# A two-layer encoder trunk on one core: the values' product ahead of the stick-breaking q and k, transposes issued in three steps, the last sparse heads two steps later

## The chip, the core and the metric

The kernel runs on one core of a Trainium2 chip. Its engines work side by side, each through its own queue of instructions in order: TensorE (PE in the profile, with its weight loads as PEld), VectorE (DVE), ScalarE (ACT), GpSimd (POOL) and SyncE (SP, which here issues DMA transfers). The metric is the device time of one execution in microseconds (us).

## What is computed

Two layers. In each, one input projection feeds three mixers over the 256 tokens: forgetting attention (fox, 6 heads), stick-breaking attention (sb, 5 heads) and sparse attention (dsa, 5 heads, whose keys an indexer with 8 heads selects). Sigmoid gates merge them, a projection and a feed-forward part follow. Cut to what matters here:

```python
h = x @ w_in[i]
(fq, fk, fv, ff_logit, sq, sk, sv, dq, dk, dv, iq, ik, iw, g) = split_cols(h)
o_fox = fox_attention(fq, fk, fv, log_f)
o_sb = stick_breaking_attention(sq, sk, sv)
dq, dk, iq, ik = (rope(a, pos) for a in (dq, dk, iq, ik))
o_dsa = dsa_attention(dq, dk, dv, iq, ik, iw)
gates = jax.nn.sigmoid(g.reshape(b, s, N_BRANCH, D_MODEL))
merged = (gates[:, :, 0] * (o_fox @ w_up_fox[i])
          + gates[:, :, 1] * (o_sb @ w_up_sb[i])
          + gates[:, :, 2] * (o_dsa @ w_up_dsa[i]))
x = layer_norm(DEEPNORM_ALPHA * x + merged @ w_out[i], ln1_g[i], ln1_b[i])
ffn = jnp.square(jax.nn.relu(x @ w_ff_in[i])) @ w_ff_out[i]
ple = jax.nn.sigmoid(x @ w_ple_gate[i]) * (p[i] @ w_ple[i])
x = layer_norm(DEEPNORM_ALPHA * x + ffn + ple, ln2_g[i], ln2_b[i])
```

## The kernel before

**Numbers in two halves.** Every operand of a product is written as a high and a low half (`split`): ScalarE rounds to the high half (L181), VectorE subtracts to get the low half (L182), or both scale on the way. A product is then three matmuls (`mm3`, L197 and the like): high by high, high by low, low by high. Weights come in units: a DMA brings a unit to a raw buffer `wr` (3 of them), the two engines split it to `wh` and `wl` (5 of each).

**Accumulators.** PSUM has eight banks: four under the name `ps`, for scores, transposes and values, and four under the name `pg`, for the products of the input projection and the up projection. `xstat` keeps the tokens still and takes two `pg` banks, one per half of the tokens (tile 0, tile 1); `wstat` keeps the weights still and takes a bank for every two blocks of 128 columns: three for `fox` (6 heads) and three for `sb` (its q and k, L407 to L410). Each name gives its banks out in a ring, so that a new accumulator waits until the bank's last content was read. When a product ends, its `done` function evacuates the banks: `c4_done` (dsa), `c3_done` (sv), `sb_done`. The first two call `do_rope`, which multiplies on VectorE into two temporary buffers, of which there are two in all (`t15`; L369, L371, L373), adds on GpSimd (L376), and splits the values after that.

**The order of the work.** `PRODUCTS` lists the products; `JOBS` lists the mixers' generators, each with the number of rounds until the next may start. In a round, every job in flight (up to FLIGHT = 6) is advanced by one step, that is, to its next `yield`; then jobs whose products are done are started, and then the products run on by about PACE = 550 columns. So a `yield` within a job puts a piece of a product between its parts. A scheduler places the instructions of each engine on from this order.

**The jobs the change touches.** `idx_T` (L485 to L497) transposes the indexer's keys and its two blocks of queries and splits them. `dsa_T` (L560 to L575) does so for the keys of the sparse heads, for four query heads in one bank, and for the fifth query head. `dsa1` and `dsa3` are `softmax_heads` for two sparse heads each: scores (L204), softmax, transposes of the weights (L217), splits, and `values` (L197 into `ps`), whose output is split into `oT` (L592, L593).

**The end of the mixers.** When all jobs are through, `zero` (L885) is computed from the last softmax tile. It is the bias of the sigmoids of the twelve gate tiles (L888), so that ScalarE loads the sigmoid's table only there. `gated` (L762) multiplies accumulators of the up projection (`up`, L758 to L831; its units `kbs` of two blocks kb) by the gates and thereby frees their `pg` banks. Then the output projection (L251) follows.

Of the kernel before, what the change touches and what calls it, by code (L numbers as in the profile page):

```python
# [27 lines left out]
BIG = 1e30  # L28
TAKEN = -3e38

PRODUCTS = ['fv', 'fox', 'iq1', 'iq2', 'dsa', 'sb', 'sv', 'g1', 'g2', 'g3', 'g4', 'g5']
JOBS = [('decay', 4), ('fox0', 2), ('fox2', 2), ('fox4', 1), ('idxT', 1), ('idx0', 3), ('idx1', 0), ('dsaT', 2), ('sb0', 2), ('sb2', 2), ('dsa0', 0), ('sb4', 2), ('dsa1', 0), ('dsa3', 4)]
PACE = 550
FLIGHT = 6
WR = 3
# [16 lines left out]
def hybrid_trunk(ctx, tc, x, p, w_in, b_forget, w_up_fox, w_up_sb, w_up_dsa, w_out,  # L52
# [10 lines left out]
    def nm(s):  # L63
        uid[0] += 1
        return f"{s}_{uid[0]}"

    def ps():
        return psp.tile([P, 512], F32, tag="ps", name=nm("ps"), bufs=4)
# [109 lines left out]
    def split(src, hi, lo, scale=None):  # L178

        if scale is None:  # L180
            a = nc.scalar.copy(hi, src)  # L181
            b = nc.vector.tensor_sub(lo, src, hi.bitcast(F32))  # L182
            if pinned[0]:
                pinned[0] -= 1
                tc.keep_in_program_order(a)
                tc.keep_in_program_order(b)
        else:
            nc.scalar.activation(hi, src, AF.Copy if isinstance(scale, float) else AF.Identity,
                                 scale=scale)
            nc.vector.scalar_tensor_tensor(lo, src, scale, hi.bitcast(F32),  # L190
                                           op0=ALU.mult, op1=ALU.subtract)
# [166 lines left out]
    for l in range(L):  # L358
# [126 lines left out]
        def idx_T():  # L485
            q = ps()
            for t in range(2):
                nc.tensor.transpose(q[:, t * P:(t + 1) * P], rnk[t][:, 0:128], ident)
            split(q[:, 0:256], *ikT)
            for g in range(2):  # L490
                q = ps()
                for b in range(2):
                    for t in range(2):
                        nc.tensor.transpose(q[:, b * T + t * P:b * T + (t + 1) * P],
                                            rnq[t][:, (2 * g + b) * P:(2 * g + b + 1) * P], ident)
                split(q, *iqT[g])
            yield  # L497
# [62 lines left out]
        def dsa_T():  # L560
            q = ps()
            for t in range(2):
                nc.tensor.transpose(q[:, t * P:(t + 1) * P], rnk[t][:, 128:256], ident)
            split(q[:, 0:256], *dkT)
            q = ps()
            for b in range(2):
                for t in range(2):
                    nc.tensor.transpose(q[:, b * T + t * P:b * T + (t + 1) * P],
                                        rnd[t][:, b * P:(b + 1) * P], ident)
            split(q, *dqT, scale=-SCALE)  # L570
            q = ps()
            for t in range(2):
                nc.tensor.transpose(q[:, t * P:(t + 1) * P], rnd[t][:, 256:384], ident)
            split(q[:, 0:256], *dq4, scale=-SCALE)
            yield  # L575
# [264 lines left out]
        for c in range(1, 6):  # L840
            products[f"g{c}"] = (KB, 512, lambda c=c: gate(c))

        jobs = {"decay": (("fv",), lambda: decay()), "idxT": (("iq1", "iq2"), idx_T),
                "idx0": (("iq1", "iq2"), lambda: idx_scores(0)),
                "idx1": (("iq1", "iq2"), lambda: idx_scores(1)),
                "dsaT": (("dsa", "sv"), dsa_T)}
        for h in (0, 2, 4):
            jobs[f"fox{h}"] = (("fox", "fv"), lambda h=h: fox_heads(h))
# [7 lines left out]
        def gemm():  # L856
            for name in PRODUCTS:
                _, n, f = products[name]
                for _ in f():
                    yield n  # L860
                emitted.add(name)

        units, todo, more = gemm(), list(JOBS), True
        while more or todo or flight:
# [181 lines left out]
```

## Time and profile before

| what | us |
|---|---|
| three runs, lowest, median, highest | 884.89, 891.12, 891.59 |
| profiled execution, its own time | 887.57 |
| its span in the trace | 885.9 |
| TensorE busy | 859.0 (97% of the span) |
| VectorE busy | 643.3 (73%) |
| ScalarE busy | 475.7 (54%) |
| GpSimd busy | 72.0 (8%) |
| mean granted clock of TensorE | 0.993 of full speed |

The span is the time from the first to the last instruction of the profiled execution; 1.7 us lie around it. Busy shares are means over the whole span. The granted clock is 1.00 at 2.4 GHz and 0.50 at 1.2 GHz. TensorE's busy time counts a matmul from its start to its modelled end, so that neighbours overlap.

### The profile page before, as it was taken

The numbers are of one execution on the slowest core, as the hardware profiler recorded it, in microseconds if no ns is written. First come the engines' busy times: TensorE is split into PE (matmuls) and PEld (weight loads), VectorE is DVE, ScalarE is ACT, GpSimd is POOL, SyncE is SP. The second block draws the span as 40 slices with busy tenths as digits, with TensorE's granted clock in tenths as the row PEclk, the third lists the DMA queues.
The fourth block names the chain that finished last, engine by engine and source line by source line (L and its number), as shares of the span: only waits on it lengthen the run. The fifth ranks groups of instructions, "written<-read, shape, count | busy, mean of one in ns | idle before, by whom it ended". The sixth has DMA issues, their size and how long they took to land. (4 is left out here: it accounts for less than half of the span.)

```text
span 885.9 us, 12952 instructions
## 1 busy us (share of the span) xinstructions
PE 859.0 (97%) x4678; PEld 733.3 (83%) x4678; DVE 643.3 (73%) x1133; ACT 475.7 (54%) x749; POOL 72.0 (8%) x138
## 2 busy tenths in 40 slices
PE   7998999999999999999999989999999999999996
PEld 5998978788788888888879988887887888888885
DVE  5588897779867666666776799967798686666665
ACT  4555657676445444444455556676844554444440
POOL 2012011100011000000000122001001010000100
PEclk9999999999999999999999999999999999999998
DMA  7654566543556666666546547554355666566751
GB/s 232 196 149 124 160 183 187 157 154 117 177 186 208 215 190 190 190 214 213 156 119 201 145 128 198 160 173 149 106 192 188 179 205 210 191 189 188 230 179 48
DMA packets 79696, 154.46 MB, mean 174 GB/s; under 512 B 10096, under 2 KB 25456, under 8 KB 79632
## 3 DMA queue, kind: packets, MB, share of 16 engines
q1 hardware_dynamic: 77952, 149.04, 55.0%
q0 software_dynamic: 1680, 4.60, 1.9%
q8 instruction: 37, 0.61, 0.3%
q14 instruction: 27, 0.22, 0.1%
HBM read 152.30 MB, written 1.05 MB: 173 GB/s over the span
## 5 line engine op out<-in xcount | busy, mean ns | idle before, releaser
L182 DVE TENSOR_TENSOR wl<-wr,wh 128x1024 fp32r<-128x1024 f32 (+5 forms) x303 | 344.2, 1142 | 185.8 <-ACT wh L181 183.1
L181 ACT CAST wh<-wr 128x1024 fp32r<-128x1024 f32 (+5 forms) x303 | 296.2, 983 | 298.3 <-PE pg L197 83.3
L197 PE MATMUL pg<-wh,t16k 128*128 128x512 f32 (+4 forms) x768 | 224.6, 367 | 0.1
L945 PE MATMUL ps<-t16k,wh 128*128 128x512 f32 x512 | 181.4, 398 | 0.0
L197 PE MATMUL pg<-wh,t2k 128*128 128x512 f32 x544 | 172.8, 394 | 1.7 <-ACT wh L181 1.4
L197 PEld LDWEIGHTS pg<-wh,t16k 128*128 128x128 f32 x768 | 140.6, 189 | 20.0 <-DVE t2k L190 0.7
L947 PE MATMUL ps<-t16k,wl 128*128 128x256 f32 x512 | 143.7, 281 | 0.0
L197 PE MATMUL pg<-wl,t16k 128*128 128x512 f32 (+4 forms) x384 | 139.5, 363 | 0.0
L197 PEld LDWEIGHTS pg<-wh,t2k 128*128 128x128 f32 x544 | 102.9, 189 | 24.2 <-ACT wh L181 1.8
L945 PEld LDWEIGHTS ps<-t16k,wh 128*128 128x128 f32 x512 | 96.2, 188 | 23.8
L197 PE MATMUL pg<-wl,t2k 128*128 128x512 f32 x272 | 106.7, 392 | 0.0
L947 PEld LDWEIGHTS ps<-t16k,wl 128*128 128x128 f32 x512 | 96.7, 189 | 0.6
L197 PEld LDWEIGHTS pg<-wl,t16k 128*128 128x128 f32 x384 | 72.7, 189 | 8.1
L197 PEld LDWEIGHTS pg<-wl,t2k 128*128 128x128 f32 x272 | 51.5, 189 | 10.9 <-DVE wl L182 0.5
L407 PE MATMUL pg<-t16k,wh 128*128 128x256 f32 x176 | 51.3, 291 | 3.7 <-DVE t16k L182 3.7
L409 PE MATMUL pg<-t16k,wh 128*128 128x256 f32 x176 | 50.5, 287 | 0.0
L410 PE MATMUL pg<-t16k,wl 128*128 128x256 f32 x176 | 50.4, 286 | 0.0
L251 PE MATMUL pg<-wh,t16k 128*128 128x512 f32 x96 | 37.6, 398 | 1.3 <-ACT t16k L181 1.2
L251 PE MATMUL pg<-wl,t16k 128*128 128x512 f32 x96 | 37.9, 399 | 0.8 <-DVE wl L182 0.6
L407 PEld LDWEIGHTS pg<-t16k,wh 128*128 128x128 f32 x176 | 34.3, 195 | 4.3 <-issue 4.1
L197 PE MATMUL pg<-wh,t1k 128*128 128x512 f32 x112 | 37.2, 396 | 0.0
L410 PEld LDWEIGHTS pg<-t16k,wl 128*128 128x128 f32 x176 | 34.5, 196 | 0.0
(180 smaller groups left out, 969.5 us busy)
## 6 DMA issues: line engine op xcount, KB each, us to landing
wr<-in_w_ff_in_dram SPq DMA_DIRECT2D x64, 512.0 KB, 4.4
wr<-in_w_ff_out_dram SPq DMA_DIRECT2D x64, 512.0 KB, 4.2
wr<-in_w_in_dram SPq DMA_DIRECT2D x48, 512.0 KB, 4.0
wr<-in_w_in_dram SPq DMA_DIRECT2D x32, 384.0 KB, 3.4
wr<-in_w_out_dram SPq DMA_DIRECT2D x16, 512.0 KB, 4.1
wr<-in_w_ple_gate_dram SPq DMA_DIRECT2D x16, 512.0 KB, 4.5
wr<-in_w_in_dram SPq DMA_DIRECT2D x16, 256.0 KB, 3.4
wr<-in_w_in_dram SPq DMA_DIRECT2D x8, 390.0 KB, 3.7
```

The source lines that it names most:

```text
L181: a = nc.scalar.copy(hi, src)
L182: b = nc.vector.tensor_sub(lo, src, hi.bitcast(F32))
L197: nc.tensor.matmul(o, l, r, start=start and i == 0, stop=stop and i == 2, skip_group_check=skip)
L251: nc.tensor.matmul(o[t][:, :n], tok(aT, u * nk + kk, t)[0], wt[i][:, kk, :], start=u + kk + i == 0, stop=False)
L407: nc.tensor.matmul(oi, hi, rh, start=kb == 0 and i % 2 == 0, stop=False, skip_group_check=True)
L409: nc.tensor.matmul(oi, hi, rl, start=False, stop=False, skip_group_check=True)
L410: nc.tensor.matmul(oi, lo, rh, start=False, stop=kb == KB - 1, skip_group_check=True)
L945: nc.tensor.matmul(pz[i], hi, x1_both[:, kb, :], start=kb == 0, stop=False, skip_group_check=True)
L947: nc.tensor.matmul(pz[i][:, 0:T], lo, x1T[0][:, kb, :], start=False, stop=kb == KB - 1, skip_group_check=True)
```

## The change

`PRODUCTS` puts `sv` (the stick-breaking values, with the first query head of the sparse mixer behind them) ahead of `sb` (the stick-breaking q and k). `idx_T` and `dsa_T` get two more `yield`s each, so that each of their three transposed banks is a step of its own. In `JOBS` two rounds instead of one lie between `idxT` and `idx0`, and two instead of none between `dsa1` and `dsa3`. Nothing else changes; lines after the new ones move by one to three (L494 is L495 after, L573 is L576, L593 is L596, L762 is L765, L779 is L782, L888 is L891).

```diff
--- before.py
+++ after.py
@@ -28,8 +28,8 @@
 BIG = 1e30
 TAKEN = -3e38
 
-PRODUCTS = ['fv', 'fox', 'iq1', 'iq2', 'dsa', 'sb', 'sv', 'g1', 'g2', 'g3', 'g4', 'g5']
-JOBS = [('decay', 4), ('fox0', 2), ('fox2', 2), ('fox4', 1), ('idxT', 1), ('idx0', 3), ('idx1', 0), ('dsaT', 2), ('sb0', 2), ('sb2', 2), ('dsa0', 0), ('sb4', 2), ('dsa1', 0), ('dsa3', 4)]
+PRODUCTS = ['fv', 'fox', 'iq1', 'iq2', 'dsa', 'sv', 'sb', 'g1', 'g2', 'g3', 'g4', 'g5']
+JOBS = [('decay', 4), ('fox0', 2), ('fox2', 2), ('fox4', 1), ('idxT', 2), ('idx0', 3), ('idx1', 0), ('dsaT', 2), ('sb0', 2), ('sb2', 2), ('dsa0', 0), ('sb4', 2), ('dsa1', 2), ('dsa3', 4)]
 PACE = 550
 FLIGHT = 6
 WR = 3
@@ -488,6 +488,7 @@
                 nc.tensor.transpose(q[:, t * P:(t + 1) * P], rnk[t][:, 0:128], ident)
             split(q[:, 0:256], *ikT)
             for g in range(2):
+                yield
                 q = ps()
                 for b in range(2):
                     for t in range(2):
@@ -562,12 +563,14 @@
             for t in range(2):
                 nc.tensor.transpose(q[:, t * P:(t + 1) * P], rnk[t][:, 128:256], ident)
             split(q[:, 0:256], *dkT)
+            yield
             q = ps()
             for b in range(2):
                 for t in range(2):
                     nc.tensor.transpose(q[:, b * T + t * P:b * T + (t + 1) * P],
                                         rnd[t][:, b * P:(b + 1) * P], ident)
             split(q, *dqT, scale=-SCALE)
+            yield
             q = ps()
             for t in range(2):
                 nc.tensor.transpose(q[:, t * P:(t + 1) * P], rnd[t][:, 256:384], ident)
```

**First place: sb's third accumulator in layer 0.** On TensorE before; `pg_1087`, `pg_1088` and `pg_1089` are the three banks of sb, `ps_1138` is the second block of the indexer's queries.

```order
L494 MATMUL ps_1138<-ident,t2k_302 128x128
L494 MATMUL ps_1138<-ident,t2k_303 128x128
L494 MATMUL ps_1138<-ident,t2k_302 128x128
L407 MATMUL pg_1089<-t16k_195,wh_1093 128x256
L409 MATMUL pg_1089<-t16k_195,wh_1093 128x256
L410 MATMUL pg_1089<-t16k_195,wl_1094 128x256
L494 MATMUL ps_1138<-ident,t2k_303 128x128
L407 MATMUL pg_1087<-t16k_195,wh_1148 128x256
```

On TensorE in the changed kernel; sb's banks are `pg_1226` to `pg_1228`, `ps_1257` is the indexer's second block of queries, and L204 are the first scores of the indexer.

```order
L217 MATMUL ps_1251<-ident,t3k_1008 128x128 x3
L495 MATMUL ps_1257<-ident,t2k_302 128x128
L495 MATMUL ps_1257<-ident,t2k_303 128x128
L495 MATMUL ps_1257<-ident,t2k_302 128x128
L495 MATMUL ps_1257<-ident,t2k_303 128x128
L407 MATMUL pg_1228<-t16k_195,wh_1232 128x256
L409 MATMUL pg_1228<-t16k_195,wh_1232 128x256
L410 MATMUL pg_1228<-t16k_195,wl_1233 128x256
L204 MATMUL ps_1265<-t1k_308,t2k_310 128x128
L204 MATMUL ps_1266<-t1k_308,t2k_310 128x128
```

Before, the last accumulator of sb is opened among the transposes of the second query block; after, behind all of them, and the indexer's scores stand right behind the unit's last matmuls.

On VectorE before, at the evacuation that this accumulator waits for; `pg_919` is the bank of tile 0 of the dsa product:

```order
L625 TENSOR_SCALAR t3k_1008<-t3k_1008,small_1118 128x128
L625 TENSOR_SCALAR t3k_1008<-t3k_1008,small_1118 128x256
L369 TENSOR_TENSOR t_212_1059<-pg_919,rope 128x64
L371 TENSOR_TENSOR t_213_1060<-pg_919,rope 128x32
L373 TENSOR_TENSOR t_213_1060<-pg_919,rope 128x32
L182 TENSOR_TENSOR wl_1261<-wr_1257,wh_1260 128x640
L182 TENSOR_TENSOR t16k_210<-pg_919,t16k_210 128x64
```

On VectorE in the changed kernel; `pg_1087` and `pg_1088` are the two banks of the sv product there:

```order
L369 TENSOR_TENSOR t_240_1206<-pg_1087,rope 128x64
L371 TENSOR_TENSOR t_241_1207<-pg_1087,rope 128x32
L373 TENSOR_TENSOR t_241_1207<-pg_1087,rope 128x32
L369 TENSOR_TENSOR t_242_1216<-pg_1088,rope 128x64
L371 TENSOR_TENSOR t_243_1217<-pg_1088,rope 128x32
L373 TENSOR_TENSOR t_243_1217<-pg_1088,rope 128x32
L182 TENSOR_TENSOR wl_1384<-wr_1380,wh_1383 128x640
L182 TENSOR_TENSOR t16k_210<-pg_1087,t16k_210 128x320
L182 TENSOR_TENSOR t16k_210<-pg_1088,t16k_210 128x320
L182 TENSOR_TENSOR t3k_1174<-ps_1251,t3k_1173 128x384
L182 TENSOR_TENSOR t2k_313<-ps_1257,t2k_312 128x512
```

Before, tile 0's value split (`t16k_210`) is the last of this row. After, the ropes of both tiles come first, then the low half of a weight unit, then both value splits, then the split of a softmax tile, and last that of the indexer's second query block.

**Second place: the end of the mixers in layer 0.** On ScalarE before; `wh_...` are the high halves of weight units, `t3k_...` those of softmax tiles, and `small_2337` is `zero`.

```order
L181 CAST wh_2423<-wr_2419 128x1024
L181 CAST t3k_2245<-ps_2282 128x384
L181 CAST t3k_2253<-ps_2288 128x384
L181 CAST wh_2442<-wr_2439 128x1024
L888 ACT_TABLE_LOAD
L888 ACTIVATE t2k_259<-t2k_259,small_2337 128x512
L181 CAST t1k_334<-ps_2315 64x256
```

On ScalarE in the changed kernel:

```order
L181 CAST t1k_334<-ps_2280 64x256
L181 CAST wh_2442<-wr_2439 128x1024
L181 CAST t3k_2291<-ps_2320 128x384
L181 CAST wh_2477<-wr_2474 128x1024
L891 ACT_TABLE_LOAD
L891 ACTIVATE t2k_259<-t2k_259,small_2337 128x512
L181 CAST t1k_336<-ps_2326 64x256
```

Before, one weight unit (`wh_2442`) is rounded between the last softmax tile and the table load; after, one stands ahead of the last softmax tile and another (`wh_2477`) behind it. That one takes the buffer of `wh_2357`.

On TensorE before, the matmuls of the up projection there; `pg_2307` and `pg_2308` are its second pair of accumulators, `pg_2383` and `pg_2384` its third, which kb = 6 opens:

```order
L197 MATMUL ps_2326<-t3k_2253,t16k_210 128x2x128
L197 MATMUL pg_2307<-wh_2357,t1k_330 128x512
L197 MATMUL pg_2307<-wl_2358,t1k_330 128x512
L197 MATMUL pg_2307<-wh_2357,t1k_331 128x512
L197 MATMUL pg_2308<-wh_2357,t1k_330 128x512
L197 MATMUL pg_2308<-wl_2358,t1k_330 128x512
L197 MATMUL pg_2308<-wh_2357,t1k_331 128x512
L779 MATMUL pg_2307<-wh_2357,t1k_332 128x512
L780 MATMUL pg_2307<-wl_2358,t1k_332 128x512
L779 MATMUL pg_2308<-wh_2357,t1k_332 128x512
L780 MATMUL pg_2308<-wl_2358,t1k_332 128x512
L779 MATMUL pg_2383<-wh_2379,t1k_333 128x512
```

On TensorE in the changed kernel, `pg_2312` and `pg_2313` are the second pair, `pg_2383` is again the first of the third:

```order
L197 MATMUL ps_2326<-t3k_2291,t16k_210 128x512
L782 MATMUL pg_2312<-wh_2357,t1k_332 128x512
L783 MATMUL pg_2312<-wl_2358,t1k_332 128x512
L782 MATMUL pg_2313<-wh_2357,t1k_332 128x512
L783 MATMUL pg_2313<-wl_2358,t1k_332 128x512
L197 MATMUL ps_2326<-t3k_2292,t16k_210 128x512
L197 MATMUL ps_2326<-t3k_2291,t16k_210 128x512
L197 MATMUL ps_2326<-t3k_2291,t16k_210 128x2x128
L197 MATMUL ps_2326<-t3k_2292,t16k_210 128x2x128
L197 MATMUL ps_2326<-t3k_2291,t16k_210 128x2x128
L782 MATMUL pg_2383<-wh_2379,t1k_333 128x512
```

Before, all values of the last heads (`ps_2326`) stand ahead of the last matmuls of the second pair; after, most of them stand between those and the third pair, and `wh_2357` is read last at the fourth row of this piece.

## Rows read from the trace of the kernel before

**Rows 1.** Windows, both mixer stretches: busy us (instructions) per engine, clock, DMA share, GB/s.

```profile
55.00:252.00 197.00, 190.96 (x1091) 162.17 (x1090) 163.23 (x360) 118.49 (x211) 23.52 (x41) 0.99 0.54 160
489.00:690.00 201.00, 195.67 (x1119) 166.58 (x1118) 165.57 (x364) 122.24 (x217) 23.63 (x41) 0.99 0.53 158
```

**Rows 2.** Waits of TensorE: line, releaser, us in total, times, longest us.

```profile
PE pg L407 <- DVE t16k L182: 3.7, 2, 1.9
PE ps L204 <- DVE t1k L593: 3.1, 2, 1.5
PE ps L573 <- DVE t1k L182: 2.0, 2, 1.2
...
PE pg L251 <- DVE wl L182: 0.6, 2, 0.4
```

**Rows 3.** Timeline, sb's third accumulator, layer 0: start, us, [idle before <-releaser].

```profile
81.25 0.28 PE L410 MATMUL pg<-t16k,wl 128*128 128x256 f32 x1
81.37 0.49 PE L217 MATMUL ps<-ident,t3k 128*128 128x128 f32 x3
...
81.92 0.93 PE L494 MATMUL ps<-ident,t2k 128*128 128x128 f32 x7
84.67 0.36 PE L407 MATMUL pg<-t16k,wh 128*128 128x256 f32 x1 [1.83 <-DVE t16k L182]
```

**Rows 4.** Windows around three clock levels, columns as in rows 1.

```profile
85.67:89.08 3.41, 3.41 (x18) 3.41 (x17) 2.61 (x8) 1.95 (x5) 1.70 (x5) 0.50 0.31 89
521.00:524.50 3.50, 3.50 (x32) 3.50 (x31) 3.04 (x11) 2.61 (x5) 1.88 (x6) 1.00 0.39 98
611.32:614.73 3.41, 3.41 (x9) 2.67 (x8) 3.34 (x20) 2.68 (x12) 0.00 (x0) 0.50 0.71 219
```

**Rows 5.** Timeline at the last sparse scores of layer 0.

```profile
174.87 0.77 DVE L593 TENSOR_TENSOR t1k<-ps,t1k 64x256 fp32r<-64x256 f32 x2
...
175.35 0.32 PE L204 MATMUL ps<-t1k,t2k 64*128 64x128 f32 x1 [1.54 <-DVE t1k L593]
```

**Rows 6.** Timeline at the end of layer 0's mixers.

```profile
192.53 0.39 PE L197 MATMUL pg<-wh,t1k 128*128 128x512 f32 x1
...
192.76 2.25 PE L197 MATMUL ps<-t3k,t16k 128*128 128x512 f32 x12
...
193.00 1.05 ACT L181 CAST wh<-wr 128x1024 fp32r<-128x1024 f32 x1 [1.60 <-issue]
194.07 1.28 ACT L888 ACT_TABLE_LOAD   x1
...
195.37 0.72 ACT L888 ACTIVATE t2k<-t2k,small 128x512 f32<-128x512 f32 x1
...
196.12 0.69 DVE L762 TENSOR_TENSOR t2k<-pg,t2k 128x512 f32<-128x512 f32 x1 [0.81 <-ACT t2k L888]
...
197.35 0.39 PE L780 MATMUL pg<-wl,t1k 128*128 128x512 f32 x1
...
197.79 0.50 PE L779 MATMUL pg<-wh,t1k 128*128 128x512 f32 x1
```

**Rows 7.** Timeline at the end of the sv product, layer 0.

```profile
111.73 0.51 PE L197 MATMUL pg<-wh,t16k 128*128 128x384 f32 x2
...
112.08 0.33 PE L197 MATMUL pg<-wl,t16k 128*128 128x384 f32 x1
...
113.17 0.21 DVE L369 TENSOR_TENSOR t<-pg,rope 128x64 f32<-128x64 f32 x1
...
113.67 1.22 POOL L376 TENSOR_TENSOR t2k<-t,t 128x64 f32<-128x64 f32 x1 [5.75 <-DVE t L373]
...
114.63 0.48 DVE L182 TENSOR_TENSOR t16k<-pg,t16k 128x320 fp32r<-128x320 f32 x1
...
115.26 0.18 DVE L373 TENSOR_TENSOR t<-pg,rope 128x32 f32<-128x32 f32 x1
```

**Rows 8.** VectorE by line and shape: count, busy us, mean ns, idle before.

```profile
L182 DVE TENSOR_TENSOR wl<-wr,wh 128x640 fp32r<-128x640 f32 x24 | 19.3, 819 | 3.9 <-ACT wh L181 3.9
```


## The prediction

> **What bounds the kernel now.** First I read the windows of the two stretches that hold the token mixers, since every moved instruction lies there [rows 1]. TensorE is busy 190.96 of 197 us in the first layer and 195.67 of 201 us in the second. The reader should see two things: TensorE sets the pace, and all its gaps together are 6.0 + 5.3 = 11.3 us. The change neither adds nor removes a matmul, so it can only act on those gaps, on the clock, and on new gaps. Next the list of who TensorE waits for [rows 2]: the third accumulator of the stick-breaking product (L407) waits 3.7 us in two pieces, the sparse scores (L204) 3.1 us in two, the last transposes of the sparse heads (L573) 2.0 us in two, and the output projection (L251) 0.6 us in two. One piece of each lies in each layer. These are the entries that the change touches. Last the clock: it falls to 0.50, the 1.2 GHz level, for 3.41 us twice [rows 4]. Once is just after the 1.83 us wait of the first layer and once just after the second layer's wait of the sparse scores; after the second layer's accumulator wait, the longer one with 1.9 us [rows 2], the stretch from 521 to 524.5 shows 1.00. A fall costs half its length, 1.7 us.
>
> **The change part by part.** All numbers are per layer first, then for both layers.
>
> *The accumulator wait.* Four banks serve the products. In the order before, sb follows dsa and its third accumulator is the bank of dsa's first token tile, whose evacuation (c4_done) is stuck in VectorE's queue: TensorE has twelve transposes between (81.37 to 82.9) and then stands 1.83 us [rows 3]. With sv ahead of sb, that bank has had a whole product's time; the whole 3.7 us goes. But sb's third accumulator is now the bank of sv's first token tile, and the same kind of wait can come back behind c3_done. I work it out from the evacuation of sv as it stands now [rows 7]: the first of three rope operations of tile 0 begins at 113.17, and the last of tile 1's three begins at 115.26 and takes 0.18, so both tiles take 2.27 us, because the temporary buffers are held by GpSimd's addition (1.22 us). In the new order on VectorE the ropes of tile 1 stand ahead of the weight half (0.82 us [rows 8]) and of tile 0's value half (0.48 us). So tile 0's bank is free at 2.27 + 0.82 + 0.48 = 3.57 us after the first rope. TensorE's cover from tile 0's last matmul is 6 matmuls at 0.175 (111.73 to 112.08 holds two) = 1.05, 12 at 0.12 (81.25 to 81.37) = 1.4, and 7 transposes at 0.11 (five from 81.37 to 81.92) = 0.8 us: 3.25. That leaves 0.3 us if VectorE begins at once; it is likely a few tenths late, and just behind stand the indexer scores, which need the second query half that VectorE splits last in that row of work. I take 1.0 us. The low end is 0 (GpSimd quick), the high end 2.1 (a wait as now, with the query half on top). Both layers: -3.7 + 2.0.
>
> *Transposes of the sparse heads in three steps.* The third transposes now wait for a bank that the first split must clear; split apart by steps, that wait goes: -2.0 us for both layers [rows 2]. In the new order the first stick-breaking scores stand right behind these third transposes, and the second head's bank waits for the split of exactly that tile; only six score matmuls and one weight matmul lie between. Also the first gate product now follows sb and its second accumulator waits for the split of sb's first bank. The nearest row for both is the one removed, 1.2 us at its longest; the floor is 0. I take 0.7 us for the two together, near the middle since more work lies between than there was: +1.4 for both layers (0 to 4).
>
> *Transposes of the indexer in three steps.* It moves the query transposes into the sv product and sb. The transposes themselves, five at 0.55 us [rows 3], cost the same anywhere; what they wait for is in the first term. Nothing else.
>
> *The last sparse heads two steps later.* Today their scores are issued right behind those of the heads before them and need two banks that VectorE must still clear (174.87, 0.77 us for two): TensorE stands 1.54 us ahead of 175.35 [rows 5]. Two steps later the banks are long free: -3.1 us for both layers. The price is in the tail. The last softmax tile feeds `zero`, behind which come the table load, the sigmoids and the gating that frees accumulators for kb = 6 of the up projection. Today, on ScalarE, the last weight cast ahead of the table load begins at 193.00, 0.47 us after the start of the matmul that frees its buffer (192.53); the load runs from 194.07 to 195.35, the first sigmoid begins at 195.37, and the first gating (196.12, 0.69 us) ends at 196.81, 3.81 us after the cast began [rows 6]. TensorE has matmuls for it up to the one of 197.35 and then waits only 0.2 us (to 197.79, less a step of 0.23). In the new order one more weight cast stands ahead of the table load, and its buffer is freed by a matmul only seven rows ahead of kb = 6: four steps of 0.23 (192.53 to 192.76) and three of 0.12 make 1.3 us of cover. The chain is 0.47 + 3.81 + 0.06 for the semaphore between engines, a choice of mine that carries little, = 4.34 us. TensorE then stands 3.04 us, less the 0.2 it waits today: +2.85, so +5.7 for both layers. It could be 2.2 if VectorE's half of the softmax tile already holds TensorE up among the seven, or 3.6 if a weight is late.
>
> *A rule that speaks against it.* The rows show the first sigmoid 0.02 us behind the end of the 1.28 us table load [rows 6]. The Trainium skill (ScalarE: Activation LUTs, What ACT_TABLE_LOAD costs) gives the load 1283 ns and a drain of about 1380 ns on top for each change of set. The trace agrees on the first figure and shows no such drain; with it the two tails would be 2.8 us longer and the time 2.8 us more than the forecast.
>
> *Weights of the output projection.* One cast that today waits behind twelve sigmoids is made ahead of them, so the projection's weights come a little earlier. At most the 0.6 us of [rows 2] goes; I take half, -0.3.
>
> *Clock.* Two falls today. The short waits that preceded them shrink, but an idle of 3 us is longer than any of those, of which two in four were followed by a fall; I count one fall in each tail, so 0 in sum (from -3.4 with none to +3.4 with four).
>
> **Sum.** -3.7 + 2.0 - 2.0 + 1.4 - 3.1 + 5.7 - 0.3 + 0 = 0.0 us. The profiled execution took 887.57 us (span 885.9 and 1.7 around it); the median of the three runs shown, 891.12, is 3.5 above it, and the lowest run 2.7 below. I take the middle of profiled time and median, 889.3 us, as the forecast: no change. What a measurement of this kernel can tell from no change is about 1%, 8.9 us.
>
> **The rivals.**
> 1. *The tail stays covered: faster.* If the added cast does not hold the table load (its buffer freed and its weights there sooner than I read from the order), the 5.7 us do not come, nor two falls of the clock: 887.6 - 5.7 - 3.4 = 878.5, on the scale of the forecast 880.3. For it: today the same chain costs 0.2 us. Against: the cast reuses the buffer of a unit that TensorE is still reading seven rows ahead of kb = 6, and an engine keeps its queue's order.
> 2. *VectorE becomes the bound behind sb: slower.* With sv ahead, sv's evacuation, the query splits, the indexer's first accumulation and eight weight halves of 0.82 us all fall into the sb product, and every product boundary there waits for a split on VectorE. Today VectorE is busy 163.23 of 197 us over the stretch [rows 1], which is 83%, and the wait of 1.83 us shows that its queue decides at such boundaries. It decides once its backlog at the first gate product passes the 2.5 us that TensorE has between sb's first bank and that bank's next use (nine matmuls at 0.12 and six at 0.23). Price: the upper ends of the first two terms instead of my values, 2 x (2.1 + 2.0 - 1.7) = +4.8, and two more falls, +3.4: 895.8, on the scale of the forecast 897.5. Against it: five weight buffers let TensorE run on while VectorE is late.
> 3. *Table load with the drain that the Trainium skill gives*: 889.3 + 2.8 = 892.1. Against it are the two sigmoids that begin at once.
>
> **How the numbers follow.** Forecast 0.66, first rival 0.13, second 0.14, third 0.02, the rest 0.05 for what I have not seen. The range of 8 in 10 reaches toward both rivals and takes in the ends of the terms and the spread of the runs, 882 to 896 us. Faster by over 1% (under 882.2) is most of the first rival, 0.09; slower by over 1% (over 900.0) the upper part of the second, 0.06; within 1% 0.85.
>
> **What would show it right or wrong.** In the list of waits of the changed kernel the L573 entry (now L576) and the L593 releaser are gone. A new entry of about 3 us per layer stands at the up projection, with the gating (L765) as releaser, behind a table load that begins just after a weight cast. At sb's third accumulator about 1 us is left in each layer, between the bank and the indexer scores. The clock falls twice, both times near the end of a mixer stretch. If the tail entry is missing, the first rival holds; if the L190 split holds TensorE for over 2 us a layer or weights (`wl`) do, the second. The forecast is wrong most easily in the tail, where one order of two instructions on ScalarE carries 5.7 us, and in the first term, where VectorE's backlog is an estimate.

## The result: 0.9% slower, and the profile after

The changed kernel took 895.77 us (median of 7 runs), the kernel before 888.1 us on the same chip (7 runs): ratio 1.0093 with a 95% interval of 1.0067 to 1.012. The profiled executions took 895.77 and 887.57 us, 8.2 us apart. The forecast of 889.3 us, no change, was too low by 6.5 us.

The list of who TensorE waits for in the changed kernel; line, releaser, us in total, times, longest:

```profile
PE pg L782 <- DVE t2k L765: 5.4, 2, 2.7
...
PE pg L407 <- DVE t16k L182: 3.0, 2, 1.6
PE ps L217 <- DVE t3k L716: 2.0, 2, 1.0
...
PE pg L251 <- ACT t16k L181: 1.4, 3, 0.8
PE ps L197 <- DVE t3k L740: 1.4, 2, 0.7
...
PE pg L197 <- DVE t2k L190: 1.0, 2, 0.6
...
PE ps L204 <- DVE t1k L190: 0.4, 2, 0.2
```

Of the entries of [rows 2] the sparse scores (3.1), the last sparse transposes (2.0) and the weights of the output projection (0.6) are gone; the third accumulator keeps 3.0 of 3.7. New are the gating (5.4), the second gate accumulator and the second stick-breaking head (1.0 and 0.4), and two that the prediction does not have: transposes (L217) that wait for a subtraction of the stick-breaking heads (L716), 2.0, and values (L197) that wait for the low half of their weights (L740), 1.4. The lists' totals are 18.2 us before and 22.5 after.

The windows of the clock's falls in the mixers of the changed kernel, columns as in [rows 1]: three, where [rows 4] has two. Each lasts 3.41 us at 0.50, the 1.2 GHz level.

```profile
200.86:204.27 3.41, 3.41 (x9) 2.65 (x9) 2.48 (x5) 3.41 (x7) 0.00 (x0) 0.50 0.04 14
535.37:538.78 3.41, 3.41 (x18) 3.41 (x18) 2.04 (x6) 1.38 (x3) 0.00 (x0) 0.50 0.53 156
641.18:644.59 3.41, 3.41 (x10) 2.63 (x9) 2.48 (x5) 3.41 (x7) 0.00 (x0) 0.50 0.01 5
```

**The tail.** The timeline of the changed kernel at the end of layer 0's mixers, against [rows 6]:

```profile
195.08 0.40 PE L782 MATMUL pg<-wh,t1k 128*128 128x512 f32 x1
...
195.56 1.05 ACT L181 CAST wh<-wr 128x1024 fp32r<-128x1024 f32 x1 [1.35 <-PE pg L782]
...
195.61 1.09 PE L197 MATMUL ps<-t3k,t16k 128*128 128x512 f32 x5
196.63 1.28 ACT L891 ACT_TABLE_LOAD   x1
...
197.92 0.72 ACT L891 ACTIVATE t2k<-t2k,small 128x512 f32<-128x512 f32 x1
...
198.67 0.69 DVE L765 TENSOR_TENSOR t2k<-pg,t2k 128x512 f32<-128x512 f32 x1 [0.81 <-ACT t2k L891]
...
199.42 0.50 PE L782 MATMUL pg<-wh,t1k 128*128 128x512 f32 x1 [2.72 <-DVE t2k L765]
```

The reader should follow it upwards. TensorE stands at 199.42 for the gating, which waits for the sigmoid, this for the table load, this for the cast at 195.56, and this for the matmul of 195.08 that reads its buffer last. From 195.08 to 199.42 are 4.34 us, the length that was forecast. The wait in it is 2.72 us, not 3.04, since the matmuls in between lasted longer than the 1.3 us put for them. The load ends at 197.91 and the sigmoid begins at 197.92. The Trainium skill (ScalarE: Activation LUTs, What ACT_TABLE_LOAD costs) gives a drain of about 1380 ns on top of the load; this trace does not show it either.

**The stick-breaking heads.** The timeline of the changed kernel at the transposes behind the last stick-breaking head, layer 0:

```profile
154.15 0.57 ACT L387 COPY t2k<-pg 128x512 f32<-128x512 f32 x1
...
155.05 0.57 ACT L387 COPY t2k<-pg 128x512 f32<-128x512 f32 x1
...
155.51 2.00 ACT L181 CAST wh<-wr 128x1024 fp32r<-128x1024 f32 x2
...
156.60 1.23 DVE L182 TENSOR_TENSOR wl<-wr,wh 128x1024 fp32r<-128x1024 f32 x1 [2.17 <-ACT wh L181]
...
157.74 0.55 DVE L715 SCALAR_TENSOR_TENSOR t3k<-ps,t3k 128x384 f32<-128x384 f32 x1
...
158.54 0.54 DVE L716 SCALAR_TENSOR_TENSOR t3k<-ps,t3k 128x384 f32<-128x384 f32 x1
...
159.23 0.52 PE L217 MATMUL ps<-ident,t3k 128*128 128x128 f32 x3 [1.02 <-DVE t3k L716]
```

The transposes take the bank that held the head's scores, and L716 reads it last. On ScalarE the two copies of a finished gate (L387) stand ahead of a weight cast; its low half (156.60 to 157.83) therefore reaches VectorE just ahead of L715 and L716. That the copies are the cause is tried below.

### The profile page after: what moved, and what is told of

It is laid out like the page before. It is cut to its first block, busy times and chain, and to the rows that moved or that the text cites. A ratio compares the mean times of both kernels' runs of the same rounds, so it can differ in the third digit from the quotient of the medians.

```text
span 894.0 us, 12936 instructions
## 1 busy us (share of the span) xinstructions
PE 863.1 (97%) x4678; PEld 736.9 (82%) x4678; DVE 645.1 (72%) x1133; ACT 474.0 (53%) x749; POOL 78.2 (9%) x138
## 4 chain that ended last, share of the span: by engine, by line
PE 74%; DVE 12%; ACT 5%; issue 4%; DMA 2%; POOL 2%; SPq 0%; POOLq 0%; DVEq 0%; ACTq 0%
PE pg L197 38%; PE ps L948 13%; PE ps L950 7%; PE pg L251 4%; DVE wl L182 4%; PE pg L256 2%; DMA wr<-in_w_in_dram 2%; ACT wh L181 2%; PE pg L407 2%; PE pg L409 2%; PE pg L410 2%; PE ps L204 1%; DVE sc L536 1%; PE ps L197 1%; DVE small L535 1%
## 5 line engine op out<-in xcount | busy, mean ns | idle before, releaser
L197 PE MATMUL pg<-wh,t16k 128*128 128x512 f32 (+4 forms) x768 | 224.1, 365 | 1.0 <-DVE t2k L190 1.0
L197 PE MATMUL pg<-wh,t2k 128*128 128x512 f32 x544 | 172.5, 393 | 1.6 <-ACT wh L181 1.4
L197 PEld LDWEIGHTS pg<-wh,t16k 128*128 128x128 f32 x768 | 139.9, 188 | 21.4 <-DVE t2k L190 1.8
L197 PE MATMUL pg<-wl,t16k 128*128 128x512 f32 (+4 forms) x384 | 138.9, 362 | 0.0
L197 PEld LDWEIGHTS pg<-wh,t2k 128*128 128x128 f32 x544 | 102.8, 189 | 24.3 <-ACT wh L181 1.8
L197 PE MATMUL pg<-wl,t2k 128*128 128x512 f32 x272 | 106.6, 392 | 0.0
L197 PEld LDWEIGHTS pg<-wl,t16k 128*128 128x128 f32 x384 | 72.2, 188 | 8.1
L197 PEld LDWEIGHTS pg<-wl,t2k 128*128 128x128 f32 x272 | 51.5, 189 | 10.6 <-DVE wl L182 0.2
L197 PE MATMUL pg<-wh,t1k 128*128 128x512 f32 x112 | 39.9, 418 | 0.0
L251 PE MATMUL pg<-wh,t16k 128*128 128x512 f32 x96 | 37.9, 399 | 1.5 <-ACT t16k L181 1.4
L251 PE MATMUL pg<-wl,t16k 128*128 128x512 f32 x96 | 37.6, 395 | 0.4 <-DVE small L294 0.3
```

What stands on the lines that cost most here:

```text
L197: nc.tensor.matmul(o, l, r, start=start and i == 0, stop=stop and i == 2, skip_group_check=skip)
L251: nc.tensor.matmul(o[t][:, :n], tok(aT, u * nk + kk, t)[0], wt[i][:, kk, :], start=u + kk + i == 0, stop=False)
```

## The experiments

All twelve were timed against the kernel before on the same chip, whose median there was 888 to 889 us.

**Late heads alone, in the kernel before.**

```diff
-('dsa1', 0)
+('dsa1', 2)
```

> The kernel before with one number changed: two rounds between the last two pairs of sparse heads. Three theories on the 3.4 us that the changed kernel waits inside the stick-breaking heads (2.0 at their neighbours' transposes, L217, and 1.4 at their values, L197). Theory A, phase: the stick-breaking heads start one round (24 gate matmuls) earlier against the gate products, and the evacuation of a gate falls into their chain; here they start where they did before, so these two waits are absent. Theory B, cover: the later last heads take matmuls away that used to lie between those steps; then the 3.4 us show here too. For the tail my prediction's step expects a wait of 2.7 us in each layer, for the gating, behind a weight cast and the table load. The accumulator wait of 3.7 and that of the last transposes of 2.0 stay, the sparse scores' 3.1 goes. A: 888.1 - 3.1 + 5.4 + 1.7 for one more fall of the clock = 892.1 us, B: 895.5 us. If the tail is not the late heads' doing: 885.

Measured 891.88 us, ratio 1.0036 (1.0017 to 1.0055). Its waits:

```profile
PE pg L779 <- DVE t2k L762: 5.8, 2, 2.9
...
PE ps L573 <- DVE t1k L182: 2.8, 2, 1.9
```

Theory A met: the gating's wait is there in full, the scores' 3.1 us is gone, and nothing waits for the stick-breaking subtractions. Theory B falls. That A's sum of 892.1 us came out is in part luck: the last sparse transposes wait 2.8 us in place of 2.0 and values that wait for a softmax tile's low half 2.1 in place of 0.9, which A does not have, and the clock falls once (522.74), not three times. Behind the gating's waits of 2.91 us, which end at 200.08 and 636.97, it does not fall:

```profile
196.00:206.00 10.00, 7.09 (x33) 5.72 (x32) 6.64 (x11) 9.68 (x15) 0.00 (x0) 1.00 0.22 80
...
632.00:642.00 10.00, 7.09 (x33) 5.75 (x32) 6.45 (x11) 8.79 (x14) 0.00 (x0) 1.00 0.28 103
```

**The changed kernel without late heads.**

```diff
-('dsa1', 2)
+('dsa1', 0)
```

> The changed kernel with no rounds between the last two pairs of sparse heads, as before. The tail's step: its waits of 2 x 2.7 us go, and with them the clock's fall behind each (3.4 us), the sparse scores' wait of 3.1 us is back. Theory A (phase): the waits inside the stick-breaking heads (2.0 and 1.4 us) stay, 895.8 - 5.4 - 3.4 + 3.1 = 890.1 us. Theory B (cover): they go too, 886.7 us. A price that neither counts: here one weight unit more is rounded only behind the twelve sigmoids, which could hold the up projection.

Measured 899.44 us, ratio 1.0127 (1.0093 to 1.0161): not faster than the changed kernel, where both theories had it faster (the profiled executions took 895.72 and 895.77 us). The gating's wait is gone and the two waits in the stick-breaking heads stay (2.1 and 1.4), as A has it, but a price that neither theory has in its sum decides:

```profile
PE ps L217 <- DVE x L301: 6.1, 4, 2.7
...
PE ps L217 <- DVE t3k L716: 2.1, 2, 1.0
PE pg L251 <- DVE wl L182: 1.7, 5, 0.4
PE ps L197 <- DVE t3k L740: 1.4, 2, 0.7
```

L301 is the end of the normalisation behind the output projection; its wait was 0.9 us before. The mixers end earlier here, one more weight unit is rounded behind the twelve sigmoids, and the output projection waits for weights in five places. That this is what makes the normalisation late was not tried apart.

**The changed kernel, stick-breaking heads one round later.**

```diff
-('dsaT', 2)
+('dsaT', 3)
```

> The changed kernel with three rounds instead of two between the sparse heads' transposes and the first stick-breaking heads, so that these start after 60 gate matmuls, as in the kernel before, and not after 36. Theory A (phase): the two waits inside the stick-breaking heads (2.0 at L217 and 1.4 at L197) go: 895.8 - 3.4 = 892.4 us, with the tail's 2 x 2.7 us still there. Theory B (cover): nothing changes there, 895.8 us. A third, C: the waits belong to the transposes in steps, which are still in steps here: 895.8 us as well.

Measured 892.15 us, ratio 1.0043 (1.0024 to 1.0062), where A said 892.4. No entry for L716 or L740 is left in its list; the gating's 5.8 us stays, and the values that wait for a softmax tile's low half wait 2.7 us in place of 1.1. Its profiled execution took 895.14 us, 3 above the median; there the clock is at 0.50 for 17.1 us in the mixers, against 10.2 in the changed kernel. Its timeline at the same place:

```profile
160.91 1.04 ACT L181 CAST wh<-wr 128x1024 fp32r<-128x1024 f32 x1
...
161.98 1.23 DVE L182 TENSOR_TENSOR wl<-wr,wh 128x1024 fp32r<-128x1024 f32 x1 [1.34 <-ACT wh L181]
...
164.85 0.54 DVE L716 SCALAR_TENSOR_TENSOR t3k<-ps,t3k 128x384 f32<-128x384 f32 x1
...
165.55 0.51 PE L217 MATMUL ps<-ident,t3k 128*128 128x128 f32 x3
```

No gate ends there, the weight half is done at 163.21, and L716 ends at 165.39, 0.16 us ahead of the transposes: even here the place has little slack. So C falls, and A holds.

**The swap alone, in the kernel before.**

```diff
-'dsa', 'sb', 'sv'
+'dsa', 'sv', 'sb'
```

> The kernel before with the values' product ahead of the stick-breaking q and k and nothing else. The stick-breaking heads then start after 12 gate matmuls, half a gate earlier than in the changed kernel and a whole gate earlier than before, so at the phase of before. Theory A (phase): no waits at L217 and L197 inside these heads; theory C or a swap that does it by itself: 3.4 us there. The third accumulator of stick-breaking q and k stands here without transposes ahead of it, so its wait is longer than the 1.5 us a layer of the changed kernel, by the cover of seven transposes (0.8 us): 2.3 a layer. The table load stands ahead of all late weight casts, so no wait for the gating. 888.1 - 3.7 + 4.6 = 889 us by A, 892.4 by the other.

Measured 895.3 us, ratio 1.0068 (1.0041 to 1.0095). Both forecasts missed. The accumulator waits 2.2 us (1.1 a layer, not 2.3), but the transposes behind the stick-breaking heads wait 2.2 too (0.6 and 1.7), although the heads stand at the phase of before; the scores keep their 3.1 and the last sparse transposes 3.0. In the second layer the subtraction is late there behind a small split that waited for a weight cast, without a gate's end nearby. So A in its strict form, that the phase alone decides, is too narrow: the place has little slack, and here a weight cast in front of it cost as much. Neither forecast has the waits behind the mixers: the normalised x (L301) 2.7 us in place of 0.9, the output projection's tokens (L251, ScalarE) 2.4 in place of 1.2.

**Swap and steps at the places of before.**

```diff
-('dsaT', 2) ... ('dsa1', 2)
+('dsaT', 3) ... ('dsa1', 0)
```

> The kernel with three rounds between the sparse transposes and the stick-breaking heads, and with no rounds between the last two pairs of sparse heads: the swap and the transposes in steps alone, at the places of before. The tail's step (the late heads put a weight cast between the last softmax tile and the table load): the gating's wait of 2 x 2.9 us goes, and the clock's falls behind it (3.4 us), the sparse scores' wait of 3.1 us is back: 892.15 - 5.8 - 3.4 + 3.1 = 886.1 us. The rival, that without late heads the weights come late behind the twelve sigmoids, as they did in the changed kernel without late heads: 892 us or more, with waits at the output projection and the transposes of the normalised x.

Measured 888.56 us, ratio 1.0014 (0.9994 to 1.0034). The gating's wait is gone and the scores' 3.1 us is back, as forecast; weights wait 1.3 us at the output projection. The median is 2.5 us over the forecast. The profiled execution is at it (886.44 us) although the clock falls once for 6.83 us (606.17), where I had counted none; what the other runs have on top stays open.

**One round between the last sparse heads.**

```diff
-('dsaT', 2) ... ('dsa1', 2)
+('dsaT', 3) ... ('dsa1', 1)
```

> Three rounds between the sparse transposes and the stick-breaking heads, and one round instead of two between the last two pairs of sparse heads. On ScalarE no weight cast then stands between the last softmax tile and the table load, while this tile is nearly as late as with two rounds. If the tail's wait is the extra cast's doing, it falls from 2.9 us a layer to what the chain of tile, zero, load, sigmoid and gating costs beyond 15 matmuls of cover, 1.1 us: 892.15 - 3.6 - 1.7 for one fall of the clock less = 886.9 us. If it is the late tile alone: 2.9 a layer and 892 us.

Measured 884.91 us, ratio 0.9976 (0.9956 to 0.9995). The gating's wait falls to 1.6 us, and the scores' wait stays away:

```profile
PE pg L782 <- DVE t2k L765: 1.6, 2, 1.1
```

In its timeline at the tail the weight cast stands ahead of the softmax tile, and the table load runs before `zero` is there:

```profile
188.71 1.06 ACT L181 CAST wh<-wr 128x1024 fp32r<-128x1024 f32 x1 [1.60 <-issue]
...
191.77 1.28 ACT L891 ACT_TABLE_LOAD   x1
...
192.30 0.16 DVE L888 TENSOR_SCALAR small<-t3k 128x1 f32<-128x1 f32 x1
...
193.06 0.72 ACT L891 ACTIVATE t2k<-t2k,small 128x512 f32<-128x512 f32 x1
```

With the cast out of the load's way 4.2 of the 5.8 us went, and the softmax tile alone, still late, costs the rest.

**The sparse transposes in steps alone, in the kernel before.** Two lines are added in `dsa_T`:

```diff
             split(q[:, 0:256], *dkT)
+            yield
...
             split(q, *dqT, scale=-SCALE)
+            yield
```

> The kernel before with the sparse heads' transposes in three steps and nothing else. My prediction's step: the wait of 2.0 us at their third transposes goes, and up to 0.7 us a layer comes at the first stick-breaking scores, which stand right behind them; the changed kernel shows 0.2 a layer there. 888.8 - 2.0 + 0.4 = 887.2 us, or 888.2 with 0.7 a layer.

Measured 886.27 us, ratio 0.9993 (0.9973 to 1.0013). The 2.0 us are gone without anything in their place at the stick-breaking scores. The gain is as large as forecast in the profiled runs (885.92 against 887.57) and too small for the interval.

**Without the copies of the third gate.**

```diff
-                nc.scalar.copy(g, o)
-                gates[c, t] = g
+                if c != 3:
+                    nc.scalar.copy(g, o)
+                gates[c, t] = g if c != 3 else gates[2, t]
```

> The changed kernel without the evacuation of the third gate product, whose two copies on ScalarE fall into the chain of the last stick-breaking head; the gating uses the second gate's tiles a second time in its place, so part of the gates is left out. If those copies are what delays that chain (they hold the cast of a weight unit, whose low half then stands on VectorE ahead of the subtraction that frees the bank for the next transposes), the wait of 1.0 us a layer at L217 goes: 895.8 - 2.0 - 1.2 for nothing else of note = 893 us at most. If the start one round earlier costs through something else, the wait at L217 stays at 1.0 a layer.

Measured 894.27 us, ratio 1.0074 (1.0044 to 1.0104). This kernel leaves one gate out and uses another in its place. The wait at L217 (its releaser's line is L717 here) falls from 2.0 to 0.4 us; the values' 1.4, the gating's 5.4 and the accumulator's 3.0 stay:

```profile
PE ps L197 <- DVE t3k L741: 1.4, 2, 0.7
...
PE ps L217 <- DVE t3k L717: 0.4, 2, 0.2
```

So those copies make most of that wait. What it is worth in time cannot be read here: the ratio's interval overlaps that of the changed kernel (1.0067 to 1.012), and in the profiled executions the clock falls once and not three times.

**The changed kernel with one round instead of two.**

```diff
-('dsa1', 2)
+('dsa1', 1)
```

> The changed kernel with one round instead of two between the last two pairs of sparse heads, and nothing else. The gating's wait falls from 5.4 us to 1.6 us, as in the kernel that also starts the stick-breaking heads a round later; the waits inside the stick-breaking heads (2.0 and 1.4 us) stay. 895.8 - 3.8 - 1.7 for one fall of the clock less = 890.3 us. The distance to that other kernel (884.9 us) is then the price of the early start, 5 us. If the early start costs only in company with the late tail: 885 us.

Measured 893.14 us, ratio 1.0064 (1.0042 to 1.0085). The two waits in the stick-breaking heads stay, 2.0 and 1.4. The gating's wait does not fall to 1.6 but is gone, and waits at the output projection and behind it stand in its place: 2.8 in place of 0.9 at the transposes of the normalised x, 2.2 and 1.3 in place of 1.4 and none at L251. The distance of 8.2 us to the kernel that differs by one round ahead of the heads is more than the 5 forecast; these waits are part of it, as in the changed kernel without late heads.

**Four rope buffers.**

```diff
-T15 = 2
+T15 = 4
```

in the kernel with three and one rounds.

> The fastest kernel so far (three rounds ahead of the stick-breaking heads, one between the last sparse heads) with four temporary rope buffers instead of two. If VectorE's wait for GpSimd between the ropes of the two tiles (0.43 us) is part of the accumulator wait of 1.4 to 1.6 us a layer, this falls by 0.4 a layer and the time to 884.0 us. If the row of work on VectorE ahead of the ropes sets it: unchanged, 884.9 us.

Measured 893.34 us, ratio 1.0061 (1.0039 to 1.0082): 8.4 us slower than with two, where nothing or a gain was expected. Not all of that is the buffers' doing: of the 6.0 us between the profiled executions (890.7 and 884.69) the lists' totals (18.2 and 16.9) give 1.3 and a further fall of the clock (99.85) 1.7, and the rest is open. The accumulator waits 4.2 us in place of 3.0, and values (L197) that wait for a split 2.5 in place of 1.4. In the order of its instructions on VectorE the ropes of both tiles of the sparse product come in a row, ahead of a softmax tile's normalisation and a weight half; with two buffers these two stood between them. That this order makes the two waits was not tried apart.

**The sparse transposes in steps and one round, no swap.**

```diff
-('dsa1', 0)
+('dsa1', 1)
```

added to the two lines in `dsa_T`.

> The kernel before with the sparse transposes in steps and one round between the last sparse heads: no swap, indexer transposes in one step. The accumulator wait of 3.7 us stays, the sparse scores' 3.1 us goes, a gating wait of 1.6 us comes: 886.3 - 3.1 + 1.6 = 884.8 us. If the swap is what makes the fastest kernel fast, this one is slower than 884.9 by the accumulator's 0.7 us and more, 886 or over; if swap and indexer steps bring nothing in sum, the two are equal.

Measured 881.67 us, ratio 0.9931 (0.9906 to 0.9956): the fastest of all, 0.7% ahead of the kernel before. Its waits:

```profile
PE pg L407 <- DVE t16k L182: 3.7, 2, 1.9
PE pg L781 <- DVE t2k L764: 1.8, 2, 1.1
```

The 3.7 us that the swap was to remove are still there. The other 3 us below the forecast fit the clock: in the profiled execution it does not fall in the mixers at all, where that of the kernel with the sparse transposes in steps alone has a fall of 6.82 us. The accumulator's wait in the second layer, by the timeline:

```profile
517.45 0.36 PE L407 MATMUL pg<-t16k,wh 128*128 128x256 f32 x1 [1.88 <-DVE t16k L182]
```

Of the two windows the first holds the first layer's wait of 1.8 us, and the second begins just behind this one:

```profile
82.00:90.00 8.00, 6.18 (x50) 5.84 (x49) 7.36 (x23) 5.05 (x12) 3.97 (x10) 1.00 0.20 52
518.00:526.00 8.00, 8.00 (x77) 7.63 (x76) 6.99 (x19) 5.62 (x11) 1.76 (x6) 1.00 0.53 141
```

**The indexer's transposes in one step.** In the kernel with three and one rounds the `yield` in `idx_T` is taken out.

> The fastest kernel so far with the indexer's transposes in one step as before (the rounds kept). The splits of the query blocks then lie ahead of the end of the sv product and not in front of its ropes on VectorE. If they are what makes the ropes start 2 us after the tile's last matmul, the accumulator wait falls from 1.5 us a layer to 0.5 or less, 883 us. If the transposes are more worth as TensorE's cover than their splits cost, it grows by their 0.8 us, to 2.3 a layer, 886.5 us.

Measured 883.03 us, ratio 0.9944 (0.9926 to 0.9963). The accumulator waits 3.0 us as with steps, now for the last rope (L373) and not for the value half, so neither theory holds. It may be that the splits ahead of the ropes and the cover of the transposes cancel out; that was not tried apart. The steps of the indexer's transposes bring nothing.

## Why the prediction was wrong

The time lies at the upper edge of the stated range (882 to 896 us), but it moved where no change was forecast; and the interval of 1.0067 to 1.012 tells a change of 0.9%, where the prediction held that less than about 1% could not be told.

**What was right.** The tail: 5.7 us net forecast, 5.4 measured less the 0.2 a layer of before, which is 5.0, by the chain that was named. Two falls of the clock followed it as forecast, but that part was luck: in the late heads alone none followed the same wait. The sparse transposes: 2.0 gone, 1.4 in their place, as put. The scores' 3.1 gone. At the output projection the 0.6 went, but its other entries grew from 1.2 to 1.7, so 0.1 was gained for 0.3 forecast. These sum to 5.0 - 0.6 - 3.1 - 0.1 = +1.2 us against 5.7 - 0.6 - 3.1 - 0.3 = +1.7 forecast.

**The step that failed** is the first one, that the change acts on the listed waits alone: "These are the entries that the change touches." The sum has the swap at the third accumulator and at the first gate product, and the stick-breaking heads only at their first scores; what an earlier start does to the rest of these heads it put at nothing. The sparse transposes need dsa and sv. With sv done ahead of sb they start while sb still runs, and so the stick-breaking heads, two rounds behind them, start a round earlier against the gates. The timeline of before shows their first scores behind the first gate's two copies, that of the changed kernel ahead of them. Before:

```profile
126.63 0.59 ACT L387 COPY t2k<-pg 128x512 f32<-128x512 f32 x1 [0.26 <-PE pg L197]
...
130.60 0.62 PE L204 MATMUL ps<-t2k,t2k 64*128 64x256 f32 x6
```

After:

```profile
122.09 0.91 PE L204 MATMUL ps<-t2k,t2k 64*128 64x256 f32 x6
...
126.47 0.58 ACT L387 COPY t2k<-pg 128x512 f32<-128x512 f32 x1
```

I compared orders at the moved instructions, not at the heads 30 us further on. That cost 3.4 us of waits (2.0 at L217, 1.4 at L197). That the early start makes both is shown by starting the heads a round later, which takes them away; that a gate's copies make most of the first is shown by leaving them out. What holds the second up was not found. The second rival's price, 897.5 us, is near the measured time, but it named the wrong place: product boundaries cost 0.7 us a layer (the 1.0 and 0.4 at L190), as in the forecast.

**The accumulator term was too small.** Left over are 1.45 and 1.6 us, not 1.0. The timeline of the changed kernel there:

```profile
89.16 0.51 PE L197 MATMUL pg<-wh,t16k 128*128 128x384 f32 x2
...
91.61 0.23 DVE L369 TENSOR_TENSOR t<-pg,rope 128x64 f32<-128x64 f32 x1
...
92.12 0.32 POOL L376 TENSOR_TENSOR t2k<-t,t 128x64 f32<-128x64 f32 x1 [2.25 <-DVE t L373]
...
92.47 0.22 DVE L369 TENSOR_TENSOR t<-pg,rope 128x64 f32<-128x64 f32 x1 [0.43 <-POOL t2k L376]
...
92.81 0.81 DVE L182 TENSOR_TENSOR wl<-wr,wh 128x640 fp32r<-128x640 f32 x1
...
93.54 0.88 DVE L182 TENSOR_TENSOR t16k<-pg,t16k 128x320 fp32r<-128x320 f32 x2
...
94.17 0.36 PE L407 MATMUL pg<-t16k,wh 128*128 128x256 f32 x1 [1.45 <-DVE t16k L182]
```

VectorE begins the ropes 2.45 us after the start of tile 0's last matmul (89.16 to 91.61), where I allowed a few tenths; from there to the free bank it needs 2.4 us, not 3.57, since GpSimd's addition took 0.32 us and not 1.22. The two errors cancel only in part.

**The clock term was too small.** I counted a fall in each tail and none at the accumulator; there was one there as well (535.37), 1.7 us.

Together 3.4 + 1.0 + 1.7 - 0.5 = 5.6 us over a forecast of no change on the profiled execution. The other 2.6 of its 8.2 us are only in part accounted for. One interruption that I worked out costs some 0.2 us more than the list says: the matmul before L217's 1.02 us wait starts at 157.82, 1.41 us ahead, and less a step of 0.23 that is 1.18. By the entries named here TensorE is interrupted twelve times where it was eight, which by that one would make 0.8 us, an estimate. What is left, under 2 us, stays open.

## What to carry to other kernels

Where a queue of jobs starts on what is finished, a swap of two producers also moves when every later job starts: count the rounds to each job against the products, and look in the trace for later places that have little slack, before costing only the instructions that were moved. Ahead of a table load look for casts that wait for a buffer; one number that takes the cast away, one round for two between the last sparse heads, brought the ratio from 1.0043 to 0.9976. Take the parts of a change one by one: here one of the four steps and half of another made the fastest kernel, and the rest brought no gain.

## What was not expected of the hardware

The clock fell after some waits and not after others of the same length: the accumulator's waits of 1.8 and 1.9 us were followed by a fall in the first layer of the kernel before, in the second layer with late heads alone, and in neither layer of the fastest kernel. The gating's waits of 2.7 to 2.9 us were followed by a fall in both layers of the changed kernel, in the second alone without the third gate's copies, and in neither with late heads alone. These are single executions: over 20 runs of the kernel before, the mean granted clock went from 0.988 to 0.998 and the time from 891.7 to 884.8 us, so the falls differ from run to run. A fall of 3.41 us costs 1.7 us and one of 6.8, as in the kernel with three and one rounds (528.49), 3.4, but whether one comes was not to be read from any row. The table load did not wait for its activation's operand: in the kernel with three and one rounds it begins 0.53 us before `zero` does.
